# RWKV-7 bonus: its multiply emitted a step later than the head-sum product

## The chip, the cores and the metric

The kernel runs on one core of a Trainium2 chip. The metric is device time in microseconds (us) of one execution. Before the change three timed runs gave 2490.37, 2496.19 and 2501.93 us, a median of 2496.19 us. One more execution was profiled; it took 2497.11 us, and the span from its first to its last instruction is 2495.4 us.

## The reference, cut to what matters

Two layers follow each other. A layer projects 1024 tokens once, splits the result among four groups of mixers (A mLSTM, B RWKV-7, C a gated linear recurrence, D retention), and maps their outputs back by one product. The change lies in B:

```python
kappa_hat = kappa * rsqrt(sum(kappa * kappa, -1) + 1e-12)
k_til = k_b * (1.0 + (a_b - 1.0) * rwkv_k_a)
wkv   = rwkv7_scan(r, w, k_til, v, kappa_hat, a)      # S_t = S_{t-1}(diag(w) - kh^T(a kh)) + v^T k_til ; y_t = S_t r_t
bonus = sum(r_b * rwkv_r_k * k_til, -1) * v_b          # a sum over the 64 channels of a head, times v
y_b   = (head_layer_norm(wkv) * gn_w + gn_b + bonus) * silu(z_b)
```

The bonus does not enter the scan. It is added to the normalised output at the very end of B's work.

## The kernel before

**Tiles of B.** B has 8 heads, taken as 4 pairs j (128 channels, two heads on 128 partitions), and each pair runs over 4 quarters qt of 256 tokens. That makes 16 tiles in a layer and 32 in the program. A quarter is 4 chunks of 64 tokens, in which the scan is rewritten as products of 64x64 matrices and the inverse of a triangular matrix.

**Three stages per tile.** `prep` (L808 to L917) loads the projected r, k and v (tile `rkv`), forms the scaled factors `AR` and `KB`, multiplies them into the chunk matrices `Gt` (L889 to L897), makes the bonus (L899 to L902), and sends the 32x32 diagonal blocks of `Gt` through DRAM (`pd`, four writes, then two reads into `Pb`, whose buffer is called `PA`; L904 to L914) so that all blocks lie on 128 partitions. `invert` (L919 to L942) inverts these blocks in a serial row of small VectorE operations on the tile `NT`, 24 scalar_tensor_tensor and 30 tensor_tensor, and writes the result to DRAM (`nd`). `mix` (L944 to L1051) reads it back, completes the inverse, runs the four chunks one after another through the state `bS`, normalises, and adds the bonus `bv` to the result `bl` (L1047).

**The bonus.** `head_sums(bps, rparts)` is a product of TensorE with a block of ones, in two parts, into one PSUM bank of the ring `bc`, which has three banks. VectorE then multiplies this bank by v into `bv`.

**What sets the order.** All stages are Python generators, the threads of a driver (`Driver.run`, L531 to L556). Each `yield STEP` ends a piece of emission. The driver keeps a model of the engines (`Clock`) and, at TensorE's modelled time, resumes the first thread whose last step has ended by the model plus 1.0 us (`SLACK`), whose condition holds, and for which two banks of its ring are free by the model; the threads stand in the order mixes, inversions and preps of B, then A and D, then C. If none can go on, it emits six matmuls of a projection piece. So TensorE's projections fill the time between the mixers' steps. The inversion's thread waits for `st["ready"] >= qt`, which `prep` sets. The framework below then orders each engine's instructions again, by priority (order of emission) and by readiness in its own model. On the chip each engine takes its instructions in the order that results. All operations are recorded by one helper, so that the profile shows L255 for each; tiles tell them apart.

The lines in question are L899 to L902 and L915 to L920:

```python
            bps = PT("bc")
            head_sums(bps, rparts)
            bv = T("bv", (128, QB))
            V.tensor_tensor(bv, bps[:, 0:QB], v, ALU.mult)
...
            ctxs[qt] = (AR, Gt, VU, Pb, bv, wc)
            yield STEP
            st["ready"] = qt

        def invert(qt):
            yield lambda: st["ready"] >= qt
```

Of the kernel before, what the change touches and what calls it, by code (L numbers as in the profile page):

```python
# [20 lines left out]
ALU = mybir.AluOpType  # L21
# [116 lines left out]
QB = 256  # L138
# [123 lines left out]
def trunk(ctx: ExitStack, tc, x, wch, wa, wd, wg, wo, pv, gb, lup, lrw, npost, cst, dtab, out):  # L262
    nc = tc.nc
    clock = Clock()
    V, A, Pl, PE, DQ = (Timed(e, n, clock) for e, n in ((nc.vector, "DVE"), (nc.scalar, "ACT"), (nc.gpsimd, "POOL"), (nc.tensor, "PE"),
                                                        (nc.sync, "SP")))
# [8 lines left out]
    def T(tag, shape, dt=F32):  # L275
        uid[0] += 1
        t = sb.tile(list(shape), dt, tag=tag, bufs=BUFS[tag], name=f"{tag}_{uid[0]}")
        if tag != "pr":
            clock.place(tag, clock.key(t), BUFS[tag])
        return t  # L280
# [16 lines left out]
    def PT(tag):  # L297
        uid[0] += 1
        t = psum.tile([128, 512], F32, tag=tag, bufs=PSB[tag], name=f"ps{tag}_{uid[0]}")
        clock.place("ps" + tag, clock.key(t), PSB[tag])  # L300
        return t
# [471 lines left out]
    def unit_b(l, P, hTs, j, drv):  # L773
        rkvd = DT(f"rkv{l}_{j}", (3, 128, S))
        st = {"p": 0, "ready": -1, "inverted": -1}
# [32 lines left out]
        def prep(qt):  # L808
# [3 lines left out]
            r, k, v = rkv[:, 0, :], rkv[:, 1, :], rkv[:, 2, :]  # L812
# [86 lines left out]
            bps = PT("bc")  # L899
            head_sums(bps, rparts)  # L900
            bv = T("bv", (128, QB))
            V.tensor_tensor(bv, bps[:, 0:QB], v, ALU.mult)  # L902

            pd = DT(f"pd{l}_{j}_{qt}", (2, MB, 32, 32))  # L904
            for b in range(2):
# [5 lines left out]
            for b in range(2):  # L911
                src = pd[b].rearrange("m s t -> m (s t)")
                DQ.dma_start(Pb[hb * b:hb * b + hb].rearrange("p s t -> p (s t)"),
                             bass.AP(tensor=src.tensor, offset=src.offset, ap=[[0, GB]] + list(src.ap)))  # L914
            ctxs[qt] = (AR, Gt, VU, Pb, bv, wc)  # L915
            yield STEP
            st["ready"] = qt  # L917

        def invert(qt):  # L919
            yield lambda: st["ready"] >= qt  # L920
# [132 lines left out]
        def preps():  # L1053
            yield lambda: st["p"] == 6 and P.lora_done

            raw = bt((128, 2, 128))
            for n in range(2):
                for part in range(2):
                    DQ.dma_start(raw[64 * part:64 * part + 64, n, :], lup[l, 64 * n:64 * n + 64, j * 128:(j + 1) * 128])
            lu = (T("luh", (128, 2, 128), F32R), T("lul", (128, 128), F32R))  # L1060
            A.copy(lu[0], raw)
            for n in range(2):
                hp = slice(64 * n, 64 * n + 64)
                V.tensor_tensor(lu[1][hp], raw[hp, n, :], lu[0][hp, n, :].bitcast(F32), ALU.subtract)
            st["lu"] = lu
            for qt in range(S // QB):
                yield from prep(qt)
# [516 lines left out]
```

## Time and profile before

| what | value |
|---|---|
| timed runs, median of 3 | 2496.19 us |
| profiled execution, its own time | 2497.11 us |
| its span | 2495.4 us |
| TensorE (PE) busy | 2354.5 us, 94% |
| VectorE (DVE) busy | 1793.1 us, 72% |
| ScalarE (ACT) busy | 1049.1 us, 42% |
| mean DMA rate | 107 GB/s |

In the trace PE is a matmul of TensorE, PEld its weight load, DVE is VectorE, ACT is ScalarE, POOL is GpSimd, SP is the engine that issues most transfers. The first layer's mixers and projections take about 62 to 1000 us of the span, its output product about 1000 to 1250 us, and the second layer repeats this from there. Tiles beginning with `pspj` are banks of the projections, `psbc` those of B's mixer, `psmx` those of A, C and D.

### The profile page before, as it was taken

To read this page: it belongs to the slowest core of one execution; us is meant where nothing else is said; L and a number is where in the kernel's file an instruction comes from. 1 tells how busy PE (TensorE), PEld (TensorE's weight loads), DVE (VectorE), ACT (ScalarE), POOL (GpSimd) and SP (SyncE) were. 2 spreads that over 40 slices of the span, in tenths; PEclk is the share of its full clock that TensorE was granted. 3 is DMA by queue.
4 is the path that set the end of the run, shared out by engine and by line. 5 is a ranking of instruction groups with operands and counts; after the bars stand their busy time and mean duration, and the time that the engine had idled before them with its cause. 6 is when DMAs were issued, how large, how long until landed. Compare 5 with 4: busy or idle time off the path is not lost.

```text
span 2495.4 us, 44964 instructions
## 1 busy us (share of the span) xinstructions
PE 2354.5 (94%) x16032; PEld 1945.6 (78%) x16032; DVE 1793.1 (72%) x5724; ACT 1049.1 (42%) x2325; POOL 196.5 (8%) x306
## 2 busy tenths in 40 slices
PE   7899999999999999999999999999999999999998
PEld 5797887787788777887777878877877887778876
DVE  6678878878878875435577787788788787754464
ACT  5333434454543553323354344335446335532233
POOL 1201000100000000000012000001001000000000
PEclk9999999999999999999999999999999999999999
DMA  5322223222223223555633232322223232236564
GB/s 162 101 74 83 64 71 102 78 76 82 91 76 82 75 90 107 184 164 180 201 117 108 61 97 65 87 88 75 77 78 95 64 92 78 87 102 223 171 204 150
DMA packets 219237, 265.82 MB, mean 107 GB/s; under 512 B 72708, under 2 KB 122244, under 8 KB 219012
## 3 DMA queue, kind: packets, MB, share of 16 engines
q1 hardware_dynamic: 210308, 254.54, 33.9%
q0 software_dynamic: 8704, 8.39, 1.4%
q8 instruction: 127, 2.08, 0.4%
q14 instruction: 98, 0.80, 0.1%
HBM read 201.76 MB, written 61.08 MB: 105 GB/s over the span
## 4 chain that ended last, share of the span: by engine, by line
PE 21%; DVE 15%; DMA 7%; issue 5%; POOL 2%; ACT 1%; SPq 1%; DVEq 0%; POOLq 0%; ACTq 0%
PE pspj L255 14%; PE psbc L255 4%; PE psmx L255 3%; DVE NT L255 2%; DVE pr L255 2%; DMA raw<-in_wo_dram 2%; DMA PA<-pd 2%; DVE lo L255 1%; DVE t L255 1%; POOL sm L255 1%; DMA rkv<-ymix 1%; DVE bS L255 1%; DVE sm L255 1%; SPq L255 1%; DVE bt L255 1%
## 5 line engine op out<-in xcount | busy, mean ns | idle before, releaser
L255 PE MATMUL pspj<-hT,hi 128*128 128x512 f32 x2880 | 937.9, 405 | 2.1 <-DVE hT L255 1.4
L255 PEld LDWEIGHTS pspj<-hT,hi 128*128 128x128 f32 x2880 | 521.0, 190 | 105.9 <-issue 2.6
L255 PE MATMUL pspj<-hT,lo 128*128 128x512 f32 x1440 | 570.0, 396 | 0.0
L255 PE MATMUL pspj<-hi,hT 128*128 128x256 f32 x2048 | 410.3, 291 | 0.0
L255 ACT CAST hi<-raw 128x512 fp32r<-128x512 f32 x372 | 229.6, 618 | 429.3 <-PE pspj L255 222.1
L255 DVE TENSOR_TENSOR lo<-raw,hi 128x512 fp32r<-128x512 f32 x372 | 257.5, 694 | 133.5 <-ACT hi L255 132.6
L255 PEld LDWEIGHTS pspj<-hi,hT 128*128 128x128 f32 x2048 | 333.8, 194 | 5.8 <-issue 1.0
L255 PEld LDWEIGHTS pspj<-hT,lo 128*128 128x128 f32 x1440 | 272.5, 189 | 59.1 <-DVE lo L255 0.2
L255 PE MATMUL pspj<-lo,hT 128*128 128x256 f32 x1024 | 293.3, 286 | 0.0
L255 PEld LDWEIGHTS pspj<-lo,hT 128*128 128x128 f32 x1024 | 199.1, 194 | 0.6
L255 POOL TENSOR_TENSOR sm<-sm,mhalf 128x4 f32<-128x4 f32 (+1 forms) x96 | 92.2, 960 | 1216.9 <-DVE sm L255 1052.2
L255 DVE SCALAR_TENSOR_TENSOR NT<-PA,NT 128x23 f32<-128x23 f32 (+15 forms) x768 | 143.1, 238 | 44.7 <-DMA PA<-pd 41.5
L255 PE MATMUL pspj<-hi,pr 128*128 128x512 f32 x384 | 131.2, 395 | 1.2 <-DVE c L255 1.2
L255 PE MATMUL psbc<-hi,pr 128*128 128x512 f32 x384 | 131.0, 395 | 0.0
L255 DVE SCALAR_TENSOR_TENSOR pr<-c,pv,pr 128x512 f32<-128x512 f32 x144 | 107.6, 747 | 14.1 <-ACT pr L255 13.4
L255 PE MATMUL psmx<-pr,t 128*128 128x65 f32 (+3 forms) x768 | 107.9, 275 | 0.0
L255 ACT ACTIVATE t<-t 128x256 f32<-128x256 f32 (+1 forms) x132 | 54.3, 411 | 123.2 <-DVE t L255 98.0
L255 PEld LDWEIGHTS psmx<-pr,t 128*128 128x128 f32 x768 | 96.8, 192 | 0.9
L255 DVE TENSOR_SCALAR bS<-psbc,wc 64x64 f32<-64x64 f32 x256 | 74.3, 290 | 28.6 <-PE psbc L255 23.4
L255 PE MATMUL psmx<-hi,pr 128*128 128x512 f32 x256 | 91.2, 397 | 2.9 <-ACT pr L255 2.0
L255 DVE TENSOR_TENSOR inv<-PA,NT 128x24 f32<-128x24 f32 (+13 forms) x480 | 87.5, 182 | 7.5
L255 DVE TENSOR_TENSOR NT<-NT,inv 128x24 f32<-128x24 f32 (+13 forms) x480 | 87.2, 182 | 6.4
(273 smaller groups left out, 3785.2 us busy)
## 6 DMA issues: line engine op xcount, KB each, us to landing
raw<-in_wch_dram SPq DMA_DIRECT2D x180, 256.0 KB
raw<-in_wo_dram SPq DMA_DIRECT2D x128, 256.0 KB
PA<-pd SPq DMA_DIRECT2D x64, 256.0 KB
zmix<-c SPq DMA_DIRECT2D x64, 256.0 KB
rkv<-ymix SPq DMA_DIRECT2D x64, 256.0 KB
rkv<-c SPq DMA_DIRECT2D x48, 256.0 KB
rkv<-rkv SPq DMA_DIRECT2D x32, 384.0 KB
lora<-lora POOLq DMA_DIRECT2D x32, 256.0 KB, 3.6
```

The source lines that it names most:

```text
L255: res = fn(*args, **kw)
```

## The change

The multiply leaves its place behind the head-sum product. It is emitted when the prep thread is resumed for the last time, behind the last `yield STEP`. The line that sets `ready` changes sides with it and now stands ahead of that yield: the inversion's thread may be resumed as soon as the prep thread has yielded, and no longer waits for the prep's step to end by the model.

```diff
             bps = PT("bc")
             head_sums(bps, rparts)
             bv = T("bv", (128, QB))
-            V.tensor_tensor(bv, bps[:, 0:QB], v, ALU.mult)
 
             pd = DT(f"pd{l}_{j}_{qt}", (2, MB, 32, 32))
...
             ctxs[qt] = (AR, Gt, VU, Pb, bv, wc)
+            st["ready"] = qt
             yield STEP
-            st["ready"] = qt
+            V.tensor_tensor(bv, bps[:, 0:QB], v, ALU.mult)
```

No instruction is added or removed. Since the driver chooses by modelled times, the order of later work moves too, on every engine.

VectorE, second tile of the first layer, from the two products that make `Gt` (written G) to the bonus multiply; sm, t and aS belong to mixer A. Before:

```order
290 L255 TENSOR_TENSOR G_1702<-psbc_1709,cst_sb 128x4x128
291 L255 TENSOR_TENSOR G_1702<-psbc_1710,cst_sb 128x4x128
292 L255 SCALAR_TENSOR_TENSOR t_1721<-pr_1395,psmx_1723 128x128
293 L255 COPY aS_99<-psmx_1723 64x65 x2
294 L255 TENSOR_TENSOR bv_1759<-psbc_1756,rkv_1347 128x256
295 L255 SCALAR_TENSOR_TENSOR t_1721<-pr_1395,psmx_1791 128x128
296 L255 TENSOR_REDUCE sm_1848<-t_1721 128x4
```

The same place in the changed program:

```order
292 L255 TENSOR_TENSOR G_1712<-psbc_1719,cst_sb 128x4x128
293 L255 TENSOR_TENSOR G_1712<-psbc_1720,cst_sb 128x4x128
294 L255 SCALAR_TENSOR_TENSOR t_1682<-pr_1395,psmx_1731 128x128
295 L255 TENSOR_REDUCE sm_1801<-t_1682 128x4
296 L255 SCALAR_TENSOR_TENSOR aS_100<-aS_99,sm_1623,psmx_1731 64x65 x2
297 L255 TENSOR_TENSOR sm_1683<-sm_1683,gT_272 128x4
298 L255 TENSOR_SCALAR sm_1801<-sm_1801 128x4
299 L255 TENSOR_SCALAR sm_1683<-sm_1683 128x4
300 L255 TENSOR_TENSOR t_1804<-t_1682,sm_1801 128x256
301 L255 TENSOR_REDUCE sm_1808<-t_1806 128x4
302 L255 TENSOR_TENSOR bv_1778<-psbc_1775,rkv_1347 128x256
```

The multiply stands 3 rows behind the second G product before and 9 rows behind it now.

VectorE, the start of the inversion of the same tile (its first row is the one with 128x31). Before:

```order
309 L255 TENSOR_TENSOR t_1868<-psmx_1869,gT_272 128x256
310 L255 TENSOR_TENSOR t_1851<-t_1851,sm_1858 128x256
311 L255 SCALAR_TENSOR_TENSOR NT_1973<-PA_1766,NT_1973 128x31
312 L255 SCALAR_TENSOR_TENSOR NT_1973<-PA_1766,NT_1973 128x23
313 L255 SCALAR_TENSOR_TENSOR NT_1973<-PA_1766,NT_1973 128x30
```

And now (TQ and bS belong to the mix stage of the tile ahead):

```order
318 L255 TENSOR_TENSOR TQ_1978<-AR_838,psbc_1980 128x2x64
319 L255 TENSOR_TENSOR TQ_1978<-cst_sb,psbc_1980 128x2x64
320 L255 TENSOR_SCALAR bS_104<-psbc_1993,wc_964 64x64 x2
321 L255 TENSOR_TENSOR pr_1871<-pr_1871,c_1872 128x8x32 x2
322 L255 SCALAR_TENSOR_TENSOR NT_1879<-PA_1784,NT_1879 128x31
323 L255 SCALAR_TENSOR_TENSOR NT_1879<-PA_1784,NT_1879 128x23
324 L255 SCALAR_TENSOR_TENSOR NT_1879<-PA_1784,NT_1879 128x30
```

Although the inversion is emitted sooner, its first row stands 29 rows behind the second G product here, and 20 rows behind it before; over the 16 tiles of a layer the mean is 15.3 rows now and 15.4 before.

VectorE, twelfth tile of the first layer, around the multiply. Before (TQ and bS belong to the mix stage of the tile ahead):

```order
1805 L255 TENSOR_TENSOR G_9027<-psbc_9035,cst_sb 128x4x128
1806 L255 TENSOR_TENSOR TQ_9058<-AR_7841,psbc_9059 128x2x64
1807 L255 TENSOR_TENSOR TQ_9058<-cst_sb,psbc_9059 128x2x64
1808 L255 TENSOR_TENSOR TQ_9058<-AR_7841,psbc_9060 128x2x64
1809 L255 TENSOR_TENSOR TQ_9058<-cst_sb,psbc_9060 128x2x64
1810 L255 TENSOR_TENSOR bv_9099<-psbc_9096,rkv_8592 128x256
1811 L255 TENSOR_SCALAR bS_104<-psbc_9073,wc_7872 64x64 x2
1812 L255 TENSOR_SCALAR bS_103<-psbc_9073,wc_7872 64x64 x2
1813 L255 SCALAR_TENSOR_TENSOR NT_9237<-PA_9106,NT_9237 128x31
```

And now; the second G product stands at row 1776 and the inversion's first row at 1785:

```order
1798 L255 SCALAR_TENSOR_TENSOR NT_8883<-PA_8880,NT_8883 128x25
1799 L255 SCALAR_TENSOR_TENSOR NT_8883<-PA_8880,NT_8883 128x17
1800 L255 SCALAR_TENSOR_TENSOR NT_8883<-PA_8880,NT_8883 128x24
1801 L255 SCALAR_TENSOR_TENSOR NT_8883<-PA_8880,NT_8883 128x16
1802 L255 SCALAR_TENSOR_TENSOR NT_8883<-PA_8880,NT_8883 128x23
1803 L255 COPY c_8989<-c_8838 128x3
1804 L255 TENSOR_TENSOR bv_8874<-psbc_8871,rkv_8510 128x256
```

Here alone (and in the same tile of the second layer) the multiply now comes behind the start of its own tile's inversion, 28 rows behind the second G product; before it stood 5 rows behind it.

## Rows read from the trace of the kernel before

**Rows 1.** The page: busy time and share of the span of each engine.

```profile
PE 2354.5 (94%) x16032; PEld 1945.6 (78%) x16032; DVE 1793.1 (72%) x5724; ACT 1049.1 (42%) x2325; POOL 196.5 (8%) x306
```

**Rows 2.** Stretches: window and its length, busy us per engine, PEclk, DMA share, GB/s.

```profile
62.50:937.50 875.00, 822.47 (x6280) 691.67 (x6279) 698.07 (x2435) 386.65 (x896) 82.75 (x122) 0.99 0.29 82
937.50:1000.00 62.50, 62.49 (x406) 49.66 (x405) 34.07 (x106) 24.25 (x47) 1.41 (x3) 1.00 0.35 106
1312.50:2187.50 875.00, 824.67 (x6349) 692.71 (x6347) 697.85 (x2420) 390.68 (x901) 82.80 (x122) 0.99 0.30 82
2187.50:2250.00 62.50, 62.49 (x419) 49.93 (x417) 32.64 (x107) 20.68 (x43) 1.41 (x3) 1.00 0.30 98
```

**Rows 3.** PE's waits: engine, bank <- releaser: us in total, times, longest.

```profile
PE psmx L255 <- DVE t L255: 21.0, 24, 2.1
PE psbc L255 <- DVE bS L255: 10.8, 15, 1.7
...
PE psbc L255 <- DVE KB L255: 7.8, 2, 4.8
PE psbc L255 <- ACT bl L255: 6.4, 6, 1.8
...
PE psbc L255 <- DVE G L255: 0.4, 2, 0.2
PE psmx L255 <- DVE hl L255: 0.3, 1, 0.3
```

**Rows 4.** DVE's waits around the change, same columns.

```profile
DVE NT L255 <- DMA PA<-pd: 41.5, 27, 3.9
...
DVE bv L255 <- PE psbc L255: 32.0, 25, 3.3
```

**Rows 5.** Instructions of tile bv: count, ns min/median/max, first and last start.

```profile
L255 DVE TENSOR_TENSOR bv<-psbc,rkv x32: 415/424/426, 115.3 to 2183.2; 128x256 f32<-128x256 f32 x32
```

**Rows 6.** Timeline of DVE, seventh tile: start, us, operation, count [idle <- releaser].

```profile
420.23 1.27 DVE L255 TENSOR_TENSOR G<-psbc,cst_sb 128x512 f32<-128x512 f32 x2
...
423.73 0.42 DVE L255 TENSOR_TENSOR bv<-psbc,rkv 128x256 f32<-128x256 f32 x1
...
428.83 0.46 DVE L255 COPY dS<-psmx 64x64 f32<-64x64 f32 x2 [1.62 <-PE psmx L255]
432.35 0.88 DVE L255 SCALAR_TENSOR_TENSOR NT<-PA,NT 128x31 f32<-128x31 f32 x5 [3.06 <-DMA PA<-pd]
```

**Rows 7.** Timeline of SP, the same tile: when its transfers are issued.

```profile
421.53 1.74 SPq L255 DMA_DIRECT2D pd<-G  x4
...
426.74 0.62 SPq L255 DMA_DIRECT2D PA<-pd  x1
```

**Rows 8.** Timeline of PE: a mixer product and the projection behind it.

```profile
440.92 0.49 PE L255 MATMUL psbc<-bS,TQ 128*128 128x128 f32 x2 [1.33 <-DVE bS L255]
441.17 0.70 PE L255 MATMUL pspj<-hT,hi 128*128 128x512 f32 x2
441.70 0.39 PE L255 MATMUL pspj<-hT,lo 128*128 128x512 f32 x1
441.93 0.62 PE L255 MATMUL pspj<-hT,hi 128*128 128x512 f32 x2
```

**Rows 9.** Chain that ended last, in order of time: start us, us, what.

```profile
1288.25 21.44 PE pspj L255 x94
...
1453.76 6.47 DMA PA<-pd
```

## The prediction

> **What bounds the kernel now.** I read the page first. TensorE is busy for 2354.5 of 2495.4 us, VectorE for 1793.1 [rows 1]. Then the stretches: in the two mixing stretches of 875 us TensorE is idle for 875 - 822.47 = 52.5 us and 875 - 824.67 = 50.3 us [rows 2], together 103 us, or 6%. In the 62.5 us behind each, where A, C and D have ended and B's last tile still runs beside projections, it is idle for 0.01 us. So TensorE's work is the floor, and a change of order can only move the 103 us. When projections run without a break a matmul takes 21.44 / 94 = 0.228 us [rows 9]; that is used below to turn counts into time.
>
> Next, who ends TensorE's pauses. The list has 18 entries that end on VectorE, from 21.0 us (t) to 0.3 us (hl), with a sum of 85.3 us [rows 3]. VectorE itself is idle for 2495.4 - 1793.1 = 702.3 us [rows 1]. So of one us that VectorE idles about 85.3 / 702.3 = 0.12 us shows on TensorE. I use this ratio wherever a wait of VectorE comes or goes. Two of its waits belong to the change: 32.0 us ahead of the bonus multiply, in 25 of 32 tiles, and 41.5 us for the blocks read back into PA, in 27 tiles [rows 4].
>
> **The multiply itself.** It runs 32 times at 424 ns [rows 5], 13.6 us of VectorE before and after; no work is gained or lost. Its place is: over a layer it stood on average 4.6 rows behind the second G product and now stands 6.9 rows behind it, counted in the order of instructions. Two of these rows are seen in the second tile, 3 and 9. A row of VectorE takes on average 1793.1 / 5724 = 0.313 us [rows 1], so 2.3 rows give the product of ones 0.7 us more. The mean wait is 32.0 / 25 = 1.28 us, so about 25 x 0.7 = 17.5 us of VectorE's waiting is covered by other work. On TensorE that is 17.5 x 0.12 = -2.1 us. Bounds: 0, if what was behind the multiply was not urgent, and -32.0 x 0.12 = -3.8 us if all of it is covered.
>
> **The inversion, emitted sooner.** This is the larger part of the edit, though the title does not name it: `ready` is set ahead of the yield, so the inversion takes its priority directly behind the reads of PA. The seventh tile shows what governs its start. The G products end at 421.50 us, the writes of pd are issued at 421.53 and the second read of PA at 426.74, and the first row of NT starts at 432.35 after VectorE has idled 3.06 us for that read [rows 6, 7]. Of the 10.9 us from G to NT other work of VectorE fills some, and the rest is waiting. How much work lies there is read from the two orders: on average 15.4 rows before and 15.3 rows now, 4.8 us each at 0.313 us a row. So VectorE arrives at the inversion as early as it did, and the blocks land when they did: the transfers are the same and are issued behind the same G product. I take 0. Bounds: if all 41.5 us were covered, -41.5 x 0.12 = -5.0 us; if nothing were left between G and NT, 32 x 4.8 = 154 us more waiting, +18.4 us on TensorE. The rows stand by zero.
>
> In the Trainium skill, page "PSUM — Partial Sum Buffer", section "Engine vs sequencer instructions", the queues of ScalarE, VectorE and GpSimd are called strict FIFO. The trace agrees: nothing runs on VectorE in the 3.06 us ahead of NT [rows 6]. The rule speaks against the change, since an inversion that is moved up to an unfinished read holds all that stands behind it; that is the second slower case below.
>
> **B's chain runs ahead.** In the order of TensorE the last transposes of B's output in a layer (psbc<-ident,bl) had 180 projection matmuls behind them up to the output product; now they have 324. B ends 144 x 0.228 = 33 us of TensorE work sooner. That looks like a gain, but the stretch in which B's last tile runs alone beside projections had no pauses to give back [rows 2]. What ends the stretch with pauses is the last product of A, C or D: 510 projection matmuls lie behind it before, 500 now. The stretch grows by 10 x 0.228 = 2.3 us at 6%, 0.1 us a layer. I take 0. Bounds: -3.9 us for two layers, if the 33 us of mixing saved its share of pauses (33 x 6% x 2), and 0.
>
> **More changes of kind on TensorE.** Counted over the whole order, TensorE goes between float32r products and float32 ones 1090 times before and 1150 times now, 30 returns more. Behind a mixer's product two projection matmuls take 0.70 us and later two take 0.62 us [rows 8]: 0.08 us for a return, 30 x 0.08 = +2.4 us. The small product ahead is overlapped by the first of them, so the net is smaller: I take half, +1.2 us, between 0 and +2.4.
>
> **The sum** against the profiled execution's 2497.1 us (2495.4 of span and 1.7 around it): -2.1 + 0 + 0 + 1.2 = -0.9, so 2496.2 us, rounded to 2496. The median of the timed runs is 2496.2, 0.9 us below the profiled execution, so the same number stands for no change. The terms are small beside what the new order does to waits that have nothing to do with B, which I cannot sum: the list of TensorE's waits counts 141 of them, and each may move.
>
> **Rivals.** Faster: B's steps meet TensorE less often. TensorE's waits on psbc banks have 12 entries from 10.8 us (bS) to 0.4 us (G), KB and ACT bl between them, with a sum of 48.4 us [rows 3]. If the chain that now runs ahead has its answers ready when TensorE comes for them in half of these places, the time is 2497.1 - 24 - 2.1 = 2471 us. For it: the 144 matmuls, and VectorE no longer stands still for the bonus. Against: a bS step has as little TensorE work between it and the next as before, since each waits for the one ahead; only the order around it moves.
>
> Slower, first: a bank held too long. The bc ring has three banks, and the bonus holds one from its product to the multiply. In the twelfth tile of each layer the multiply stands 28 rows behind G, behind 17 rows of its own inversion, which must first see its blocks land. That is 28 x 0.313 = 8.8 us instead of 5 x 0.313 = 1.6 us, and 3.06 us more if VectorE idles for PA [rows 6]. The mix stage takes banks in pairs and a third for its output; if it needs the third in that time, TensorE stands for up to 8.8 us in each layer, 2497.1 + 17.6 = 2515 us. It decides from 12.5 us on, that is when 6.3 us of the hold are passed on in both layers. Against: two banks are left, and 30 of 32 tiles hold theirs for two rows more.
>
> Slower, second: the inversion blocks VectorE's queue. With the upper bound above, 2497.1 + 18.4 = 2515 us; it decides from 12.5 / 0.12 = 104 us of added waiting, 3.3 us in each tile. Against: the equal counts of rows between G and NT.
>
> No effect on order where it counts is part of the forecast: in the first tile the multiply moves by one row.
>
> **How the numbers follow.** About 0.5%, 12.5 us, is what a measurement of this kernel can tell from no change. The forecast, no more than that from 2496, gets 0.50. The faster rival, with any reshuffle that helps, gets 0.28; the bank 0.12 and the blocked queue 0.10, together 0.22 slower. The range for 8 in 10 reaches near the ends that were worked out on both sides: 2473 to 2513. The likeliest case alone, from its bounds (2497.1 - 3.8 - 5.0 - 3.9 and 2497.1 + 2.4) and 6 us to each side for the spread of the timed runs, is 2478 to 2506.
>
> **What would show it.** Right: TensorE's busy time within a few us of 2354.5 and its idle time in the two mixing stretches near 103 us; VectorE's wait ahead of bv down from 32.0 to about 15 us; its wait for PA near 41.5 us; TensorE pausing nowhere for bv. The last B tile should end about 33 us sooner ahead of each output product, with no gain from it. Wrong: a wait of TensorE's psbc on DVE bv or NT in the twelfth tile (the bank), a PA wait above 100 us (the queue), or psbc waits well under 48 us in total with a time below 2484 (the faster rival). A sum of waits on psmx that moves by over 12 us would mean that mixers A and D decide, for which I have no term.

## The result, and the profile after

The changed kernel takes 2521.23 us, the median of four runs (2517.99 to 2523.37). The kernel before, run beside it, takes 2494.53 us (2490.37 to 2501.93). The ratio is 1.0106, with a 95% interval from 1.0089 to 1.0122: the change makes the kernel 1.06% slower. That lies 8 us above the upper end of the range.

The profiled execution took 2517.99 us, its span is 2516.1 us, 20.7 us longer than before. The page's row of busy times, which answers to [rows 1]:

```profile
PE 2366.3 (94%) x16032; PEld 1953.1 (78%) x16032; DVE 1785.8 (71%) x5724; ACT 1048.5 (42%) x2325; POOL 196.6 (8%) x306
```

The counts are those of before. TensorE is busy for 11.8 us more and idle for 2516.1 - 2366.3 = 149.8 us, 8.9 us more than before (140.9). So the time came in two parts: new pauses, and slower work.

The stretches of [rows 2] in the changed kernel, with the same columns (window and its length; busy us of PE, PEld, DVE, ACT, POOL; granted clock, DMA share, GB/s):

```profile
62.50:937.50 875.00, 818.21 (x6302) 685.69 (x6301) 702.08 (x2485) 387.00 (x900) 83.42 (x124) 0.99 0.29 81
937.50:1000.00 62.50, 62.50 (x410) 49.92 (x409) 28.55 (x70) 23.66 (x46) 2.75 (x4) 1.00 0.31 102
1312.50:2187.50 875.00, 817.66 (x6285) 684.53 (x6283) 698.85 (x2470) 385.25 (x895) 83.34 (x124) 0.99 0.30 81
2187.50:2250.00 62.50, 62.50 (x411) 50.00 (x410) 28.22 (x68) 23.88 (x46) 2.42 (x2) 1.00 0.31 103
```

The two mixing stretches hold 56.8 + 57.3 = 114.1 us of pauses, 11 us more than before; the 62.5 us behind each still hold none.

Who ends TensorE's pauses, which answers to [rows 3] (bank, releaser: us in total, times, longest):

```profile
PE psmx L255 <- DVE t L255: 33.7, 35, 2.8
PE psbc L255 <- DVE bS L255: 14.6, 15, 1.8
PE psbc L255 <- DVE KB L255: 13.9, 6, 4.9
PE psmx L255 <- DVE pr L255: 12.3, 3, 9.8
PE psbc L255 <- DVE bl L255: 11.4, 12, 1.7
PE psmx L255 <- DVE inv L255: 9.1, 6, 2.0
...
PE psbc L255 <- ACT bl L255: 0.5, 2, 0.3
```

The largest entry, mixer results `t` of A and D, went from 21.0 us in 24 places to 33.7 us in 35. Over the whole list, the waits on psmx banks that VectorE ends grew from 47.0 us in 60 places to 60.2 us in 64 (without the one of 9.8 us at the kernel's start, which the list of before gives to a DMA). B's own, on psbc banks, grew from 35.7 to 45.9 us where VectorE ends them and fell from 12.7 to 2.5 us where ScalarE does.

VectorE's two waits that belong to the change, answering to [rows 4]:

```profile
DVE NT L255 <- DMA PA<-pd: 47.2, 25, 4.8
...
DVE bv L255 <- PE psbc L255: 13.5, 11, 2.5
```

Both came out close to the forecast: the wait ahead of the multiply fell from 32.0 to 13.5 us, and that for the blocks went from 41.5 to 47.2 us. The seventh tile, to be compared with [rows 6]: VectorE idles ahead of the inversion's first row, for the read of PA (start, us, operation, count, idle and releaser in brackets):

```profile
418.04 1.28 DVE L255 TENSOR_TENSOR G<-psbc,cst_sb 128x512 f32<-128x512 f32 x2
...
422.22 0.42 DVE L255 TENSOR_TENSOR bv<-psbc,rkv 128x256 f32<-128x256 f32 x1
...
428.90 2.25 DVE L255 SCALAR_TENSOR_TENSOR NT<-PA,NT 128x31 f32<-128x31 f32 x14 [1.23 <-DMA PA<-pd]
```

It idles 1.23 us there instead of 3.06 us. The wait that the edit moved is shorter, and yet the kernel is slower.

One of the new pauses shows how they look. TensorE in the changed kernel, around a product of mixer A:

```profile
272.58 1.15 PE L255 MATMUL psbc<-VU,G 128*64 128x64 f32 x32
276.56 0.69 PE L255 MATMUL psmx<-ident,t 128*128 128x128 f32 x2 [2.82 <-DVE t L255]
276.89 1.20 PE L255 MATMUL pspj<-hT,hi 128*128 128x512 f32 x2
```

Here no projection stands between B's product and A's, so the 2.82 us in which A's result is made have no cover. VectorE in that time:

```profile
274.11 0.23 DVE L255 SCALAR_TENSOR_TENSOR NT<-PA,NT 128x19 f32<-128x19 f32 x1
274.25 0.41 DVE L255 TENSOR_REDUCE sm<-t 128x4 f32<-128x256 f32 x1
274.58 0.23 DVE L255 SCALAR_TENSOR_TENSOR NT<-PA,NT 128x18 f32<-128x18 f32 x1
274.73 0.16 DVE L255 TENSOR_TENSOR sm<-sm,sm 128x4 f32<-128x4 f32 x1
274.85 0.24 DVE L255 SCALAR_TENSOR_TENSOR NT<-PA,NT 128x17 f32<-128x17 f32 x1
275.00 0.16 DVE L255 COPY sm<-cst_sb 128x4 f32<-128x4 f32 x1
276.07 0.42 DVE L255 TENSOR_TENSOR t<-t,sm 128x256 f32<-128x256 f32 x1 [0.91 <-POOL sm L255]
```

A's normalisation alternates with rows of the inversion and then waits 0.91 us for GpSimd. None of these rows is the bonus; three of them, 0.7 us together, are the inversion's, whose start the other line of the edit governs. The projections behind the pause also run slower, 1.20 us for two matmuls instead of 0.70 [rows 8]; the granted clock of 275 to 280 us is 0.66, and that of the 5 us before is 1.00 (rows of this kind follow in the experiments).

### The profile page after: what moved, and what is told of

Same layout as the page of the kernel before. It is cut to its first block, busy times and chain, and to the rows that moved or that the text cites. A ratio compares the mean times of both kernels' runs of the same rounds, so it can differ in the third digit from the quotient of the medians.

```text
span 2516.1 us, 44983 instructions
## 1 busy us (share of the span) xinstructions
PE 2366.3 (94%) x16032; PEld 1953.1 (78%) x16032; DVE 1785.8 (71%) x5724; ACT 1048.5 (42%) x2325; POOL 196.6 (8%) x306
## 4 chain that ended last, share of the span: by engine, by line
PE 23%; DVE 15%; DMA 7%; issue 3%; POOL 2%; ACT 1%; SPq 1%; POOLq 0%; DVEq 0%; ACTq 0%
PE pspj L255 15%; PE psbc L255 4%; PE psmx L255 4%; DVE NT L255 3%; DMA PA<-pd 2%; DVE pr L255 2%; DVE t L255 1%; DVE lo L255 1%; DMA raw<-in_wo_dram 1%; DVE bt L255 1%; POOL sm L255 1%; DVE bS L255 1%; DVE sm L255 1%; DMA t<-ga 1%; DVE inv L255 1%
## 5 line engine op out<-in xcount | busy, mean ns | idle before, releaser
L255 PE MATMUL pspj<-hT,hi 128*128 128x512 f32 x2880 | 946.8, 406 | 2.1 <-DVE hT L255 1.4
L255 PE MATMUL pspj<-hi,hT 128*128 128x256 f32 x2048 | 405.3, 290 | 0.0
L255 DVE SCALAR_TENSOR_TENSOR NT<-PA,NT 128x20 f32<-128x20 f32 (+15 forms) x768 | 140.5, 236 | 49.7 <-DMA PA<-pd 47.2
L255 ACT ACTIVATE t<-t 128x256 f32<-128x256 f32 (+1 forms) x132 | 54.3, 412 | 179.7 <-DVE t L255 158.6
```

Of the source, the lines that this page charges most:

```text
L255: res = fn(*args, **kw)
```

## The experiments

Three theories stood. **M**: the multiply's later place costs the time, through the bank or the queue. **P**: the inversion, which may now start sooner, takes VectorE from A and D just when TensorE waits for them. **R**: no step of the change costs anything by itself. The driver places every later step by modelled times, so any small change draws a new order of the whole program; the orders differ by about 1%, and the one before happens to be a good one.

Medians of the kernel before on the chips used were 2493.79, 2487.64 and 2487.18 us for the three groups of four runs below. Ratios are against these, with 95% intervals.

**The two halves of the change, each alone.** First the line that sets `ready`, with the multiply left in place:

```diff
             ctxs[qt] = (AR, Gt, VU, Pb, bv, wc)
+            st["ready"] = qt
             yield STEP
-            st["ready"] = qt
```

> The kernel before with only the line st["ready"] moved ahead of the last yield; the multiply stays behind the head-sum product. Theory P (the inversion emitted early takes VectorE from mixers A and D): as slow as the changed kernel, 2515 to 2525 us, with TensorE's waits for t and KB raised as there (33.7 and 13.9 us). Theory M (the multiply's later place costs: bank or late bonus): near 2495 us. Theory R (any new order drawn by the planner moves the time by about 1%, whatever its cause): anywhere in 2475 to 2525 us, with no tie to the sum of the parts.

Measured: 2518.2 us, ratio 1.0099 [1.0075, 1.0123]. Then the multiply alone, behind the yield, with `ready` left behind the yield too:

```diff
             bv = T("bv", (128, QB))
-            V.tensor_tensor(bv, bps[:, 0:QB], v, ALU.mult)
...
             yield STEP
             st["ready"] = qt
+            V.tensor_tensor(bv, bps[:, 0:QB], v, ALU.mult)
```

> The kernel before with only the multiply moved behind the last yield, just behind the line that sets ready, which stays where it was. Theory P: near 2495 us. Theory M: 2515 to 2525 us, with waits on psbc that end on bv. Theory R: anywhere in 2475 to 2525 us.

Measured: 2524.9 us, ratio 1.0127 [1.0103, 1.0152]. So each half costs as much as the whole, 1.0% and 1.3% against 1.06%. Costs that belong to the halves would add up; these don't. M expected waits on psbc banks that end on `bv`; with the multiply alone there are none. The largest of TensorE's waits in the first of them (`ready` alone; 21.0 us before):

```profile
PE psmx L255 <- DVE t L255: 40.1, 36, 2.8
```

That is what P expects. But with the multiply alone, where `ready` was not moved, `t` has 24.7 us and the time is longer still; the two largest of its waits:

```profile
PE psmx L255 <- DVE t L255: 24.7, 21, 2.9
PE psbc L255 <- DVE bl L255: 21.6, 13, 3.4
```

The page's row of that kernel, and the granted clock, of that kernel first and then of the kernel before:

```profile
PE 2378.4 (94%) x16032; PEld 1966.0 (78%) x16032; DVE 1795.4 (71%) x5724; ACT 1048.5 (42%) x2325; POOL 194.6 (8%) x306
```

```profile
core 0: 2522.1 us, clock 0.981
core 0: 2495.4 us, clock 0.990
```

TensorE is idle for 2522.1 - 2378.4 = 143.7 us, hardly more than before (140.9), but it is busy for 23.9 us more, with the same instructions. The mean clock says why: 0.981 against 0.990 before. The engine has 1 - 0.981 of 2522.1 us, 47.9 us, less at full rate than the span, and before it had 25.0. One place shows how it comes about. A pause of TensorE in this kernel:

```profile
738.04 0.28 PE L255 MATMUL pspj<-hi,hT 128*128 128x256 f32 x1
740.23 0.41 PE L255 MATMUL psbc<-ident,bl 128*128 128x128 f32 x2 [1.91 <-DVE bl L255]
...
741.07 0.40 PE L255 MATMUL pspj<-hi,hT 128*128 128x256 f32 x2
...
741.46 0.63 PE L255 MATMUL pspj<-hi,hT 128*128 128x256 f32 x2
```

And the windows around it (the last three columns are granted clock, DMA share and GB/s):

```profile
735.00:740.00 5.00, 3.32 (x28) 3.11 (x26) 3.96 (x15) 1.65 (x5) 1.14 (x1) 1.00 0.11 16
740.00:745.00 5.00, 4.77 (x29) 4.36 (x30) 4.87 (x14) 2.77 (x7) 0.00 (x0) 0.64 0.32 89
745.00:750.00 5.00, 5.00 (x27) 4.66 (x27) 0.00 (x0) 0.77 (x3) 0.00 (x0) 0.50 0.20 56
750.00:755.00 5.00, 5.00 (x43) 4.68 (x43) 1.98 (x3) 1.20 (x2) 0.00 (x0) 0.84 0.15 52
```

The engine pauses for 1.91 us, is busy again, and then the clock falls to 0.50, the lower level of 1.2 GHz. The same two matmuls go from 0.40 to 0.63 us, and between 745 and 750 us 27 matmuls fit where 43, of a somewhat different mix, fit in the 5 us behind. So a pause costs its own length and, sometimes, several us of half rate behind it. The Trainium skill, page "TensorE: Matmul & The Clock Gate", section "HAM oscillation — how this bites in real kernels", tells of a clock that falls back where TensorE waits for a DMA for longer than the work between two such waits takes. These rows agree in the fall and differ in what came before it: here the work ahead is long and dense, and the pause is 1.91 us.

**The multiply emitted later, the order not redrawn.** The model books the multiply at its old place, and the real instruction is emitted at the new one, so the driver's times stay as they were:

```diff
             bv = T("bv", (128, QB))
-            V.tensor_tensor(bv, bps[:, 0:QB], v, ALU.mult)
+            clock.op("DVE", "tensor_tensor", (bv, bps[:, 0:QB], v), {})
...
             st["ready"] = qt
+            nc.vector.tensor_tensor(bv, bps[:, 0:QB], v, ALU.mult)
```

> The planner's model books the multiply at its old place, and the instruction itself is emitted a step later without being booked again; ready stays behind the yield. So the driver's decisions stay closer to those of before, while the multiply stands later on VectorE. Theory M: over 2510 us. Theories P and R: near 2495 us, within 0.5%, since little else moves; its order differs from before in 6058 lines of VectorE against 9282 for the changed kernel, so that theory R allows a part of its scatter, 2483 to 2507 us.

Measured: 2492.07 us, ratio 0.9996 [0.9982, 1.0011]. Against the multiply alone, the same emission with the driver's model told of it, that is 1.3% less. The largest of its waits is near that of [rows 3]:

```profile
PE psmx L255 <- DVE t L255: 22.3, 25, 2.7
```

In the traces, 15982 of TensorE's 16032 matmuls write and read the same tiles (buffer numbers left out) at the same place of its order as before; with the multiply alone 7608 do, in the changed kernel 5356, and in the kernel before with the margin of 1.1 us tried below 5910. So with the order kept the time is kept, and with the order redrawn it moves. What this run does not show is a later multiply: the framework below sorts each queue again, and brought the multiply back to 5.3 rows behind the second G product on average, against 5.1 before and 7.2 in the changed kernel (each instruction counted; 4.6 and 6.9 in the prediction, where rows that repeat count once); VectorE's wait ahead of it is 30.8 us, nearly that of before. The run is close to the same program. That the later place holds up no bank is read elsewhere: in none of the 14 profiled kernels does an entry of TensorE's waits name `bv`, not even in the changed kernel with a margin of 1.1 us, where the multiply stands 13.1 rows behind on average and 71 at most. Nor was the line that sets `ready` tried with the order kept.

**The planner's margins, in both kernels.** If R holds, a small change of a margin that has nothing to do with the bonus moves the time as much. `SLACK` is the 1.0 us that the driver adds to a step's modelled end, `LATE` the 2.5 us by which it puts off the pieces that a mixer leaves for later (L524):

```diff
-SLACK, LATE = 1.0, 2.5
+SLACK, LATE = 1.1, 2.5
```

> The kernel before with the planner's margin SLACK at 1.1 us in place of 1.0: neither the multiply nor ready is touched, only the order is drawn anew. Theories P and M: within 0.5% of before, 2483 to 2507 us. Theory R: it moves as much as the change did, by 10 to 25 us to either side.

Measured: 2503.52 us, ratio 1.0034 [1.0017, 1.0051]: 9.7 us slower, just short of the 10 that R expected, and inside what P and M expected. The other way, 0.9, in the kernel before:

> The kernel before with the planner's margin SLACK at 0.9 us: multiply and ready untouched, order drawn anew. Theory P (the inversion emitted early takes VectorE's time from mixers A and D): within 0.5% of before, 2481 to 2506 us, TensorE's waits on psmx that VectorE ends near 47 us. Theory R (the order before is a good draw and nearly any new draw is slower): slower than before by 8 to 35 us.

Measured: 2527.14 us, ratio 1.0156 [1.0131, 1.0182], slower than the change under study, as R expected and P did not. Its granted clock is 0.983 over a span of 2525.8 us. The same two margins in the changed kernel:

> The changed kernel with SLACK at 0.9 us. Theory P: 20 to 30 us slower than the kernel before with the same SLACK, and waits on psmx ended by VectorE near 70 us. Theory R: no fixed distance to that kernel; it may be faster than it, and the waits fall on other tiles.

Measured: 2499.45 us, ratio 1.0054 [1.0034, 1.0073].

> The changed kernel with SLACK at 1.1 us. Theory P: 20 to 30 us above the 2503.5 us of the kernel before with that SLACK, and waits on psmx ended by VectorE near 70 us. Theory R: anywhere in 2485 to 2530 us.

Measured: 2517.89 us, ratio 1.0122 [1.0098, 1.0147]. At 0.9 the kernel with the change is the faster of the two by 27.7 us (2527.14 - 2499.45), at 1.1 the slower by 0.9% (by the two ratios, since these two ran on different chips). The sign of the change's effect turns with a margin of 0.1 us. Then the second margin, `LATE`, at 2.3 instead of 2.5, first in the kernel before, then in the changed one:

```diff
-SLACK, LATE = 1.0, 2.5
+SLACK, LATE = 1.0, 2.3
```

> The kernel before with the planner's delay of the output steps, LATE, at 2.3 us in place of 2.5: again only a new order. Theory P: within 0.5% of before, 2481 to 2506 us. Theory R: slower than before by 8 to 35 us.

Measured: 2483.18 us, ratio 0.9978 [0.9967, 0.999]. R expected 8 to 35 us more than before; that failed, so a new order is not always slower.

> The changed kernel with LATE at 2.3 us, the partner of the kernel before at 2.3 (2483 us). By theory R, which the last four runs favour, the order decides and not the edit: anywhere in 2485 to 2530 us. Theory P, if it is only half right: about 2510 us, 1% above its partner. In either case the span should be TensorE's work of about 2334 us plus its idle time plus half of the time at the low clock, within 8 us.

Measured: 2505.85 us, ratio 1.0082 [1.0052, 1.0112]. And at 2.7:

> The kernel before with LATE at 2.7 us. Theory R: 2483 to 2530 us, the spread of the orders seen so far. Theory P: within 0.5% of before, 2478 to 2503 us. The same sum of work, idle time and low clock should give the span within 8 us.

Measured: 2507.07 us, ratio 1.0066 [1.0041, 1.0092].

> The changed kernel with LATE at 2.7 us. Theory R: 2485 to 2530 us, with no fixed distance to the kernel before at the same LATE, of either sign. Theory P: 20 to 30 us above it.

Measured: 2507.65 us, ratio 1.0072 [1.0048, 1.0096].

All five pairs in one table, each ratio against the kernel before as it stands. The last two columns are TensorE's waits on psmx banks that VectorE ends, in us of the profiled execution, without the pause at the kernel's start:

| SLACK, LATE | without the change | with it | difference | psmx waits without | with |
|---|---|---|---|---|---|
| 1.0, 2.5 | 1 | 1.0106 | +1.06% | 47.0 | 60.2 |
| 0.9, 2.5 | 1.0156 | 1.0054 | -1.02% | 62.4 | 54.3 |
| 1.1, 2.5 | 1.0034 | 1.0122 | +0.88% | 37.2 | 48.1 |
| 1.0, 2.3 | 0.9978 | 1.0082 | +1.04% | 41.8 | 62.4 |
| 1.0, 2.7 | 1.0066 | 1.0072 | +0.06% | 38.4 | 60.5 |

The differences have a mean of +0.40% and a standard deviation of 0.90%, so the standard error of the mean is 0.40%, and with five pairs the 95% interval runs from about -0.7% to +1.5%. A cost that goes with the change at every margin is not told from zero; one as large as the +1.06% is not excluded either. Margins alone spread the kernel before from -0.2% to +1.6%. The +1.06% lies inside that.

P as a steady cost is not borne out by the same runs: it expected the changed kernel to be 20 to 30 us slower at every margin, and at 0.9 it is 27.7 us faster, at 2.7 as fast within 0.06%; at 1.1 and 2.3 the time came out as it expected, though at 1.1 with psmx waits of 48.1 us instead of about 70. The psmx waits speak for a part of P all the same. With the change they are higher in four pairs of five, by 11 to 22 us, and lower in the one in which the time is lower too. But they don't set the time by themselves: at `LATE` 2.7 they grow by 22.1 us and the time stays, with TensorE idle for 139.7 us against 139.5, since the waits on psbc banks shrink from 54.5 to 39.8 us. Whether the earlier inversion holds a part of the +1.06% stays open.

**The quiet multiply and the best margin together.** The edit that books the multiply at its old place, and `LATE` at 2.3:

> The multiply emitted a step later without being booked again, as in ghost_mult, on the order of the fastest kernel so far (before with LATE at 2.3, 2483 us). If the later multiply itself costs nothing, 2478 to 2490 us, as ghost_mult stood to before; if the multiply's place costs in an order with fewer pauses, over 2495 us.

Measured: 2483.79 us, ratio 0.9982 [0.997, 0.9994], the same as the margin alone (0.9978). So the multiply's emission gives nothing on this order either. These two are the fastest seen, some 0.2% below the kernel before; since five settings were tried, a part of that is luck of the draw. The page's row of the kernel before at `LATE` 2.3:

```profile
PE 2360.7 (95%) x16032; PEld 1952.7 (79%) x16032; DVE 1788.0 (72%) x5724; ACT 1052.3 (42%) x2325; POOL 195.7 (8%) x306
```

Its span is 2482.8 us, so TensorE is idle for 122.1 us there, 18.8 us less than before, and busy for 6.2 us more.

**One account for all.** Take from TensorE's busy time what the lower clock has cost it, span x (1 - mean clock). What is left is 2329.5 us before, 2338.6 after, 2330.5 with the multiply alone, 2324.9 at the slack of 0.9 and 2335.5 in the last run; over all 14 profiled kernels it lies between 2325 and 2342. The spans lie between 2478.2 and 2525.8, a spread nearly three times as wide. The rest is pauses (122 to 158 us) and lower clock (17 to 48 us):

| kernel | span | PE idle | lower clock | what is left |
|---|---|---|---|---|
| before | 2495.4 | 140.9 | 25.0 | 2329.5 |
| after | 2516.1 | 149.8 | 27.7 | 2338.6 |
| multiply alone | 2522.1 | 143.7 | 47.9 | 2330.5 |
| before, slack 0.9 | 2525.8 | 158.0 | 42.9 | 2324.9 |
| quiet multiply, late 2.3 | 2478.2 | 125.4 | 17.3 | 2335.5 |

The column of the lower clock is rough by some us: the mean clock has three digits, 1.2 us of such a span, and each row is one execution. The executions of the kernel before have mean clocks from 0.987 to 0.995, that is 12 to 32 us.

For the changed kernel this gives +8.9 us of pauses, +2.7 us of lower clock, and +9.1 us of TensorE's work that neither explains. Over the timed executions, with a mean clock of 0.988 in four of the changed kernel and 0.991 in 48 of the kernel before, the part of the lower clock is nearer to 7 us. Two groups of matmuls are busy for longer, the chunk products psbc<-VU,G (65.7 us instead of 60.4) and the projections pspj<-hT,hi (946.8 instead of 937.9), one for less, pspj<-hi,hT (405.3 instead of 410.3). TensorE also goes 60 times more often between kinds of product (1149 against 1089 in the traces), but that does not explain the 9.1 us: the multiply alone has 1149 of these changes as well and `ready` alone 1165, and what is left there is 2330.5 and 2331.8 us, near the 2329.5 of before. The 9.1 us stay open.

## Why the prediction was wrong

**The multiply.** The forecast took 17.5 us of VectorE's wait away; 32.0 - 13.5 = 18.5 us went. The agreement is luck, since the wait goes down in other orders without any later multiply: to 6.9 us with `ready` alone, and to 13.3 and 22.2 us in the kernel before at margins of 1.1 and 0.9. With `ready` alone:

```profile
DVE bv L255 <- PE psbc L255: 6.9, 7, 2.6
```

No pause of TensorE is seen to have gone with it: the term of -2.1 us rested on the ratio of TensorE's pauses to VectorE's idle time, 0.12, which is an average over waits of all kinds and says nothing of this one. A gain of 2.1 us could not be found among changes ten times as large.

**The inversion.** The counts of rows between G and the inversion (15.4 and 15.3) held, and so did the reading that the transfers decide: the wait for PA is 47.2 us, far from the 100 us that would have meant a blocked queue. The slower rival of the queue is refuted. What the sum did not ask is whom the inversion's rows hold up once they run: it priced VectorE's wait for the blocks, and not mixers A and D, which share VectorE with them.

**The bank in the twelfth tile.** VectorE in the changed kernel, around its multiply:

```profile
700.64 1.28 DVE L255 TENSOR_TENSOR G<-psbc,cst_sb 128x512 f32<-128x512 f32 x2
...
711.23 0.41 DVE L255 SCALAR_TENSOR_TENSOR NT<-PA,NT 128x31 f32<-128x31 f32 x2 [0.29 <-DMA PA<-pd]
...
714.69 0.42 DVE L255 TENSOR_TENSOR bv<-psbc,rkv 128x256 f32<-128x256 f32 x1
```

The multiply starts 12.8 us behind the end of the G products, more than the 8.8 + 3.1 us of the rival's sum. But no pause of TensorE is ended by `bv`, there or anywhere, so the hold was not passed on. This rival named a time, 2515 us, close to the measured one by a mechanism that is not there; that is luck.

**The faster rival.** It needed TensorE's waits on psbc banks well under 48.4 us. They are 45.9 + 2.5 = 48.4 us in the changed kernel too, so it is refuted.

**B's chain ahead.** The last transposes of B's output in the first layer begin at 999.3 us instead of 1026.6, 27 us sooner where 33 were forecast, and nothing came of it: the layer's output product starts at 1072.9 us instead of 1067.5. The step was right, and so was its value of nothing.

**The kinds of product.** 60 more changes were forecast and 60 came. Their price is of the size forecast: in the kernel before, at the full clock, a first projection product of 512 columns behind a float32 one is followed by the next after 323 ns on average, one in an unbroken row after 230, so 30 returns give at most 2.8 us. With as many changes, the multiply alone leaves TensorE 1.0 us more work than before.

**The step that failed** is the last sentence of the sum: the terms are small beside what the new order does to waits that have nothing to do with B, "which I cannot sum". What could not be summed was entered as zero, with a range of -0.9% and +0.7% around it. The margins show what it should have been. A redraw spreads the time from -0.2% to +1.6%, mostly upward, since the order that it starts from is among the better ones: of nine other orders with these margins, with and without the change, eight are slower and one is faster. The list of 141 waits was in view; their sum was taken as neutral, and from this order it is not. The prediction had the right sign to look for: psmx waits that move by over 12 us. They moved by 13.2 us.

A premise of the sum failed with it, that TensorE's work is the floor and "a change of order can only move the 103 us" of pauses. Of the 20.7 us by which the span grew, 11.8 are busy time of TensorE, with the same instructions.

One reason for that is the clock, which the sum left out. It counted a pause at its own length; the rows behind the pauses that end at 276 and 740 us show that some cost more. With the multiply alone this is nearly the whole loss (47.9 - 25.0 = 22.9 us of lower clock), in the changed kernel a smaller part of it.

## What to carry to other kernels

Where a planner with modelled times sets the order, an edit is two things: its own effect, and a new draw of everything behind it. Compare over several settings of the planner's margins rather than one. To see the edit's own effect, book the old operation in the model while emitting the new one, and look in the order that results whether the new place was kept; here it was not. From a tuned order, expect a redraw to lose about as much as unrelated margins do, and count TensorE's short pauses with what the lower clock adds behind them.

## What the runs showed of the hardware

That pauses of under 2 us are sometimes followed by the lower clock, in the midst of dense work, was not expected. In the changed kernel one more such place, TensorE first and then the windows:

```profile
1617.77 1.22 PE L255 MATMUL psmx<-pr,pr 64*128 64x128 f32 x6 [1.69 <-ACT t L255]
```

```profile
1610.00:1615.00 5.00, 5.00 (x58) 4.25 (x56) 3.33 (x10) 1.81 (x5) 1.01 (x1) 1.00 0.33 74
1615.00:1620.00 5.00, 3.31 (x21) 2.51 (x22) 4.12 (x13) 1.34 (x4) 0.00 (x0) 0.78 0.71 180
1620.00:1625.00 5.00, 5.00 (x21) 3.80 (x18) 2.78 (x13) 1.29 (x4) 0.40 (x2) 0.54 0.69 159
```

A pause of 1.69 us, ended by ScalarE, is followed by a clock of 0.78 and 0.54; 21 matmuls, of another mix, stand in a window in which 58 stood before. Not every pause of this length does it: the changed kernel has 44 pauses over 1.2 us, and its clock stands at the lower level in 13 places of the whole span. One of these is the span's end; each of the other 12 begins within a pause or shortly behind one or several. What sets apart the pauses that it follows is not shown here.
